# Both feed-forward products of a transformer step as seven block products with the middle layer in DRAM

## The chip, the cores and the metric

The kernel runs on one core of one Trainium2 chip. A core has five engines that each work through a queue of their own in order: TensorE (PE, matrix products), VectorE (DVE), ScalarE (ACT), GpSimd (POOL) and SyncE (SP), which issues the transfers between DRAM and the on-chip memory. The matrix products write to PSUM, eight banks of 512 float32 columns on each of 128 partitions. The metric is the time on the device of one run, in microseconds, median of three runs; lower is better.

## The reference

One layer of a hybrid network over 1152 tokens (128 sample tokens, then 1024 prompt tokens) of width 1024: recurrent mixers, cross attention over a memory, a feed-forward of width 4096, and a final norm. The part that matters here:

```python
def rms_norm(x, w):
    xf = x.astype(jnp.float32)
    y = xf * lax.rsqrt(jnp.mean(xf * xf, axis=-1, keepdims=True) + EPS)
    return (y * w.astype(jnp.float32)).astype(x.dtype)
```

and, in each layer, `x + squared_relu_mlp(rms_norm(x, norm_ffn_w), w_ff1, w_ff2)`, where the feed-forward multiplies by `w_ff1` (1024 x 4096), takes max(0, .) squared, and multiplies by `w_ff2` (4096 x 1024). At the end comes `rms_norm(x, norm_final_w)`.

## The kernel before

The features lie on the 128 partitions and the tokens along the free axis, in three blocks of 384 (`BW`). Every large product is made in three matmuls: each operand is split into a high part and the rest, and `mm3` adds high x high (L206), high x rest of the tokens (L207) and rest of the weights x high (L208) in PSUM. The split of a weight chunk of 128 x 1024 is a cast on ScalarE (L187) and a subtraction on VectorE (L188); `load_w` does both, and the chunk itself comes by one transfer of 512 KB (L177).

A `Driver` writes the program: it runs one stream of dense products and, between its steps, pieces of other tasks that are due. That, with the priority of some instructions, settles the order of each engine's queue before the run. Most large tiles live in 34 equal slots (`NSLOT`); a tile can only be written when its slot's last use is over.

The stages: the mixers until about 690 us, then the output projection, the attention and its projection `wo`, until about 1063 us, then the feed-forward until 1872 us, then the end of the final norm. While `wo` runs, `ffn_pre` makes the normalised input of the feed-forward block by block: `norm_split` (L1196 to L1200) multiplies by the norm's weight, splits, squares, and adds the squares on GpSimd; the factor 1/rms of each token is applied later, to the products. `ff1` multiplies one of 32 chunks of 128 features by the three blocks, and `relu2` applies the factor and max(0, .) on VectorE (L1447), squares on ScalarE (L1448) and splits the result into two slots. After every four chunks, `ff2` adds that group's part of the second product, through `ff2_unit` (L1475), to the residual in the slots `x1`. There are eight groups; the last is done by `ff2_last`, in blocks of 384, 512 and 256 tokens, with the final norm's sums (L1490, L1493) and `final` (L1507, L1512, L1514, output at L1517) behind each block. The middle layer never leaves the chip.

## Time and profile before

| | |
|---|---|
| median of three runs | 1884.41 us (1883.89 to 1886.3) |
| profiled execution, span | 1885.5 us |
| mean granted TensorE clock | 0.993 |
| TensorE busy | 1847.3 us, 98% |
| VectorE busy | 1011.8 us, 54% |
| ScalarE busy | 660.8 us, 35% |
| GpSimd busy | 224.8 us, 12% |
| moved by DMA | 167.61 MB, mean 89 GB/s |

The profile is one execution. An engine's busy time is what its instructions took; a wait is idle time before an instruction, with the instruction that released it. Matmuls overlap: one is listed with its whole length, 0.34 us at 384 columns, while the next starts sooner, so the rate is read from the starts. The granted clock is the share of TensorE's full 2.4 GHz.

### The profile page before, as it was taken

Reading aid. Unit: us, or ns where it says so; the run is one execution under the profiler, and the core shown is the slowest. Engines: PE = TensorE matmul, PEld = TensorE weight load, DVE = VectorE, ACT = ScalarE, POOL = GpSimd, SP = SyncE. Lnnn points to the kernel's source line nnn. Section 1 sums busy time; section 2 is a strip of 40 time slices with the busy share of each in tenths; the row PEclk is TensorE's granted clock in tenths of the full one; section 3 lists DMA queues with packets and bytes.
Section 4 is the critical chain, followed back from the end, with each engine's and each line's share of the span. In section 5 each row is a group of like instructions: output and inputs, shape, how many; then the busy total and the mean of one; then the engine's idle time right before and its main releaser. Section 6 shows DMA issues by size and latency. Waiting matters only on the chain.

```text
span 1885.5 us, 29978 instructions
## 1 busy us (share of the span) xinstructions
PE 1847.3 (98%) x12182; PEld 1796.4 (95%) x12182; DVE 1011.8 (54%) x2008; ACT 660.8 (35%) x1476; POOL 224.8 (12%) x262
## 2 busy tenths in 40 slices
...
DVE  6867756756756676436677533333333333333346
...
POOL 3123223123113012010012100000000000000003
...
DMA packets 73825, 167.61 MB, mean 89 GB/s; under 512 B 21680, under 2 KB 39760, under 8 KB 73688
## 3 DMA queue, kind: packets, MB, share of 16 engines
...
q14 instruction: 41, 0.34, 0.1%
q10 hardware_dynamic: 296, 0.19, 0.0%
...
## 4 chain that ended last, share of the span: by engine, by line
PE 86%; DVE 6%; ACT 3%; DMA 2%; issue 1%; POOL 1%; SPq 0%; DVEq 0%; ACTq 0%; POOLq 0%
PE d L206 25%; PE d L208 24%; PE d L207 24%; DVE y L583 1%; DVE wl L188 1%; DVE B L730 1%; DMA wr<-wout 1%; ACT xh L327 1%; DVE B L731 1%; ACT wh L187 1%; DMA R<-rowD 1%; DVE up L596 1%; PE st L960 1%; DMA xf<-xT 0%; ACT junk L672 0%
## 5 line engine op out<-in xcount | busy, mean ns | idle before, releaser
L187 ACT CAST wh<-wr 128x1024 fp32r<-128x1024 f32 x184 | 193.2, 1050 | 628.8 <-PE d L207 574.0
L206 PE MATMUL d<-xh,wh 128*128 128x384 f32 x944 | 342.3, 363 | 1.3 <-DVE k L428 0.6
L208 PE MATMUL d<-xh,wl 128*128 128x384 f32 x944 | 321.1, 340 | 0.3 <-DVE wl L188 0.3
L207 PE MATMUL d<-xl,wh 128*128 128x384 f32 x944 | 318.3, 337 | 0.0
L188 DVE TENSOR_TENSOR wl<-wr,wh 128x1024 fp32r<-128x1024 f32 x183 | 225.7, 1234 | 97.6 <-ACT wh L187 97.3
L206 PE MATMUL d<-hh,wh 128*128 128x384 f32 (+2 forms) x768 | 259.9, 338 | 0.0
L206 PE MATMUL d<-fh,wh 128*128 128x384 f32 x768 | 259.5, 338 | 0.0
L208 PE MATMUL d<-fh,wl 128*128 128x384 f32 x768 | 258.4, 336 | 0.0
L207 PE MATMUL d<-fl,wh 128*128 128x384 f32 x768 | 258.2, 336 | 0.0
L207 PE MATMUL d<-hl,wh 128*128 128x384 f32 (+2 forms) x768 | 257.9, 336 | 0.0
L208 PE MATMUL d<-hh,wl 128*128 128x384 f32 (+2 forms) x768 | 257.7, 336 | 0.0
L1475 DVE TENSOR_TENSOR x<-d,x 128x384 f32<-128x384 f32 (+1 forms) x200 | 107.5, 541 | 220.3 <-PE d L208 220.3
L206 PEld LDWEIGHTS d<-xh,wh 128*128 128x128 f32 x944 | 179.1, 190 | 7.4 <-issue 5.3
L207 PEld LDWEIGHTS d<-xl,wh 128*128 128x128 f32 x944 | 179.4, 190 | 1.6 <-issue 1.4
L208 PEld LDWEIGHTS d<-xh,wl 128*128 128x128 f32 x944 | 178.3, 189 | 0.8 <-DVE wl L188 0.6
L1447 DVE SCALAR_TENSOR_TENSOR sq<-d,rf 128x384 f32<-128x384 f32 x96 | 53.5, 558 | 174.3 <-PE d L208 171.0
L207 PEld LDWEIGHTS d<-hl,wh 128*128 128x128 f32 x768 | 144.3, 188 | 1.3
L208 PEld LDWEIGHTS d<-hh,wl 128*128 128x128 f32 x768 | 144.2, 188 | 1.4
L206 PEld LDWEIGHTS d<-hh,wh 128*128 128x128 f32 x768 | 144.2, 188 | 1.3
L207 PEld LDWEIGHTS d<-fl,wh 128*128 128x128 f32 x768 | 144.2, 188 | 0.0
L206 PEld LDWEIGHTS d<-fh,wh 128*128 128x128 f32 x768 | 144.1, 188 | 0.0
L208 PEld LDWEIGHTS d<-fh,wl 128*128 128x128 f32 x768 | 144.1, 188 | 0.0
...
## 6 DMA issues: line engine op xcount, KB each, us to landing
...
```

Source lines behind the costliest of these rows:

```text
L187: nc.scalar.copy(wh, raw)
L188: (nc.gpsimd if pool else nc.vector).tensor_tensor(wl, raw, wh, ALU.subtract)
L206: mm(ps, lhsT=lh, rhs=rh, start=start, stop=False)
L207: mm(ps, lhsT=lh, rhs=rl, start=False, stop=False)
L208: mm(ps, lhsT=ll, rhs=rh, start=False, stop=stop)
L327: nc.scalar.activation(xh, x(k), AF.Copy, scale=wc)
L583: v.scalar_tensor_tensor(y[:, :n], up[:, j:j + n], self.convw[:, c, j:j + 1], y[:, :n], ALU.mult, ALU.add)
L596: v.scalar_tensor_tensor(up[:, P:T], up[:, P:T], 1.0, y[:, 152:1176], ALU.add, ALU.mult)
L730: v.tensor_tensor(tmp[:, :, :i + 1], X[:, :, :i + 1], bc(NP[:, 0:i + 1, i], [72, 16, i + 1], 1), ALU.mult)
L731: v.tensor_reduce(X[:, :, i], tmp[:, :, :i + 1], AX.X, ALU.add)
L1447: v.scalar_tensor_tensor(r, ps[:, :BW], 0.0, self.rf[:, s], ALU.max, ALU.mult)
L1475: self.nc.vector.tensor_tensor(x, ps[:, o:o + hi - lo], x, ALU.add)
```

## The change

Both feed-forward products are cut into 2 x 2 blocks of features, of summed index and of tokens, and each set of eight block products is replaced by seven (Strassen's scheme in Winograd's form). Tokens are taken in two halves of 576, each of two quarters of 288 (`Q`). Per unit, four sums of weight blocks are made on GpSimd (`wf_sums`), and each of the seven left factors is split anew on ScalarE and VectorE (`wf_split`), three products ahead.

First layer: a unit is a pair of feature tiles. Pairs 0 to 2 are done for the first half of the tokens alone, pairs 3 to 15 for both halves, then pairs 0 to 2 for the second half: 19 units. `ff_in` makes the weighted input on ScalarE and the squares' sum on GpSimd, writes the residual to DRAM (`x2D`), and `ff_split` makes four sums of input blocks on GpSimd and seven splits for each half. A unit's seven products go to three double banks X, Y, Z of PSUM and are taken out by `evac`; `up_out` makes the four sums that the second layer wants of the hidden blocks and writes them to DRAM (`hD`), four transfers for a unit.

Second layer: a unit is a pair of output tiles, four for each of five groups of pairs (`GROUPS`). `hid_in` reads a group's hidden blocks back and splits them (L1690, L1691), as the last unit of the group before frees its slots. The residual comes back from DRAM into `E`, and every product is added to it (L1738). Pairs 14 and 15 (`PLAIN`) are kept as they are and go through `ff2_last`, whose 288 matmuls are the old ones. The final norm writes each feature tile by a transfer of its own, 32 in place of 12. `ffn_pre`, `ff1`, `relu2` and `ff2` are gone. Some constants move to a pool that ends with the mixers; before the feed-forward nothing else is changed.

The core of the diff:

```diff
+Q = 288
+HALVES = 2
+GROUPS = ((3, 4, 5), (6, 7, 8), (9, 10, 11), (0, 1, 2), (12, 13))
+PLAIN = (14, 15)
+FIRST = 3
+UP = (("P6", "s2", "T2", "Y"), ("P1", "A11", "B11", "X"), ("P5", "s1", "T1", "Z"), ("P7", "s3", "T3", "Y"),
+      ("P2", "A12", "B21", "X"), ("P4", "A22", "T4", "Y"), ("P3", "s4", "B22", "Z"))
+DOWN = (("P6", "s2", "T2", "Y"), ("P5", "s1", "T1", "Z"), ("P1", "A11", "B11", "X"), ("P3", "s4", "B22", "Z"),
+        ("P7", "s3", "T3", "Y"), ("P2", "A12", "B21", "X"), ("P4", "A22", "T4", "Y"))
...
+    def ff_in(self, b):
...
+        for k in range(KT):
+            yield from self.until(f"wo{b}{k}")
+            x = self.x1[b](k)
+            wc = self.prm[:, P_WFFN + k:P_WFFN + k + 1]
+            sq = acc if k == 0 else self.t(self.m4, [P, BW], "sq", bufs=2)
+            nc.scalar.activation(sq, x, AF.Square)
+            for q, lo, hi, to in self.pieces(b):
+                t = self.xq[q // 2][f"B{1 + k // 4}{1 + q % 2}"]
+                nc.scalar.activation(t[:, k % 4, to:to + hi - lo], x[:, lo:hi], AF.Copy, scale=wc)
+            if k:
+                nc.gpsimd.tensor_tensor(acc, acc, sq, ALU.add)
+            yield 0.0, 0.3
+        for g in range(3):
+            nc.sync.dma_start(self.x2D[:, 3 * g:3 * g + (3 if g < 2 else 2), s], self.x1g[b][g])
...
+    def ff_split(self, a):
...
+        tt = nc.gpsimd.tensor_tensor
+        tt(x["T1"], x["B12"], x["B11"], ALU.subtract)
+        tt(x["T2"], x["B22"], x["T1"], ALU.subtract)
+        x["T3"] = x.pop("B12")
+        tt(x["T3"], x["B22"], x["T3"], ALU.subtract)
+        tt(x["T4"], x["B21"], x["T2"], ALU.subtract)
+        yield 0.0, 3.0
+        for _, _, n, _ in UP:
+            yield from self.room(2)
+            h, l = self.S([P, 4, Q], F32R, "xqh"), self.S([P, 4, Q], F32R, "xql")
+            self.split(x[n], h, l)
+            self.F()
+            self.xo[a][n] = (h, l)
+            yield 0.0, 1.0
+            self.done.add(f"xo{a}{n}")
...
+    def wf_raw(self, src, n):
+        r1 = self.t(self.wp, [P, 1024], "wr")
+        r2 = self.t(self.m3, [P, 1024], "wr2", bufs=2)
+        with self.hp():
+            for r, a in zip((r1, r2), src):
+                self.nc.sync.dma_start(r[:, :2 * n], a)
+        return {"A11": r1[:, :n], "A12": r1[:, n:2 * n], "A21": r2[:, :n], "A22": r2[:, n:2 * n]}
+    def wf_sums(self, q, n):
+        def tt(o, a, b, op):
+            q[o] = self.t(self.m3, [P, 512], "ws", bufs=4)[:, :n]
+            with self.hp():
+                self.nc.gpsimd.tensor_tensor(q[o], q[a], q[b], op)
+        tt("s1", "A21", "A22", ALU.add)
+        tt("s2", "s1", "A11", ALU.subtract)
+        yield
+        tt("s3", "A11", "A21", ALU.subtract)
+        tt("s4", "A12", "s2", ALU.subtract)
+        yield
+    def wf_split(self, t, n):
+        if self.wi % 2 == 0:
+            self.wfh = self.t(self.wp, [P, 1024], "wh", F32R)
+            self.wfl = self.t(self.wp, [P, 1024], "wl", F32R)
+        o = 512 * (self.wi % 2)
+        self.wi += 1
+        h, l = self.wfh[:, o:o + n], self.wfl[:, o:o + n]
+        with self.hp():
+            self.nc.scalar.copy(h, t)
+            self.nc.vector.tensor_tensor(l, t, h, ALU.subtract)
+        return h, l
+    def seven(self, units, tasks):
...
+        for u, (_, _, products, body) in enumerate(units):
+            start(u + 1)
+            for x in tasks.get(u, ()):
+                self.dr.spawn(x)
+            next(body)
+            for j, p in enumerate(products):
+                ahead(i + 3)
+                if j in (3, 5):
+                    add(u + 1)
+                yield from body.send((p, ready[i]))
+                ready[i] = None
+                i += 1
...
+    def products(self, ps, w, x, n, blocks, first):
+        (wh, wl) = w
+        for a in blocks:
+            for k in range(n):
+                h, l = x(a, k)
+                s = slice(k * P, k * P + P)
+                self.mm3(ps[:, a, :Q], wh[:, s], wl[:, s], h, l, first and k == 0, k == n - 1, not first)
+                yield 3 * Q / 2180.0
...
+        def relu2(t, ps, n):
+            v.scalar_tensor_tensor(t, ps, 0.0, rf[:, bs, n], ALU.max, ALU.mult)
+            nc.scalar.activation(t, t, AF.Square)
+        def evac(name, o):
+            if name == "P1":
+                D, C = slot("D"), slot("C")
+                nc.scalar.copy(D[:, 1, bs], o)
+                v.tensor_tensor(C[:, 1, bs], bank["Y"][:, bs, :Q], D[:, 1, bs], add)
+            elif name == "P7":
+                B = slot("B")
+                v.tensor_tensor(B[:, 1, bs], o, H["D"][:, 1, bs], add)
+                v.tensor_tensor(H["C"][:, 0, bs], bank["Z"][:, bs, :Q], B[:, 1, bs], add)
+                relu2(H["C"][:, 0, bs], H["C"][:, 0, bs], 1)
+            elif name == "P2":
+                relu2(slot("A")[:, 0, bs], o, 0)
+            elif name == "P4":
+                v.tensor_tensor(H["B"][:, 0, bs], o, H["D"][:, 1, bs], add)
+                relu2(H["B"][:, 0, bs], H["B"][:, 0, bs], 0)
+            elif name == "P3":
+                t = H["D"][:, 0, bs]
+                v.tensor_tensor(t, o, H["C"][:, 1, bs], add)
+                relu2(t, t, 1)
+                for a in blocks:
+                    self.left[a] -= 1
+                    if not self.left[a]:
+                        self.F(14)
+                if not any(self.left):
+                    self.F()
+                    self.keep = 0
+                self.dr.spawn(self.up_out(pair, H, blocks), 0.0)
...
+    def up_out(self, pair, H, blocks):
...
+            tt = lambda o, a, b: v.tensor_tensor(o, a, b, ALU.subtract)
+            tt(A[:, 1, bs], D[:, 0, bs], A[:, 0, bs])
+            yield 0.0, 0.5
+            tt(C[:, 1, bs], C[:, 0, bs], A[:, 1, bs])
+            yield 0.0, 0.5
+            tt(D[:, 0, bs], C[:, 0, bs], D[:, 0, bs])
+            yield 0.0, 0.5
+            tt(B[:, 1, bs], B[:, 0, bs], C[:, 1, bs])
+            yield 0.0, 1.5
+            d = self.hD[pair]
+            for i, t in enumerate((C, A, D, B)):
+                q = slice(0, 1) if i == 2 else slice(0, 2)
+                nc.sync.dma_start(d[i][:, q, bs], t[:, q, bs])
...
+    def hid_in(self, g):
...
+        for i, names in ((0, ("B22", "T2")), (1, ("B11", "T1")), (2, ("T3",)), (3, ("B21", "T4"))):
+            step = 2 if i == 2 else 1
+            for j in range(0, len(pairs), step):
+                yield from self.room(3 + self.keep)
+                t = self.S([P, 2, 2, Q], F32, "ht")
+                self.live += 2
+                some = pairs[j:j + step]
+                for o, p in enumerate(some):
+                    if i == 2:
+                        nc.sync.dma_start(t[:, o], self.hD[p][2][:, 0])
+                    else:
+                        nc.sync.dma_start(t, self.hD[p][i])
+                use = [((j + o, "T3"), o) for o in range(len(some))] if i == 2 else [((j, n), o) for o, n in enumerate(names)]
+                yield 0.0, 3.5
+                self.live -= 2
+                q = len(some) if i == 2 else 2
+                h = self.S([P, 2, 2, Q], F32R, "hh")
+                l = self.S([P, 2, 2, Q], F32R, "hl")
+                nc.scalar.copy(h[:, :q], t[:, :q])
+                v.tensor_tensor(l[:, :q], t[:, :q], h[:, :q], ALU.subtract)
+                self.F()
+                for key, o in use:
+                    hid[key] = (h[:, o], l[:, o])
+                    self.done.add(f"hid{g}{key[0]}{key[1]}")
+                yield 0.0, 0.5
...
+    def down(self, g, d):
...
+            with self.hp():
+                o = bank[b][:, :, :Q]
+                e1, e2 = self.E[2 * d], self.E[2 * d + 1]
+                f1 = self.fs[d // 2][:, d % 2]
+                add = lambda e, t: v.tensor_tensor(e, e if t is f1 else t, t if t is f1 else e, ALU.add)
+                if name == "P1":
+                    if g == 0:
+                        nc.scalar.copy(f1, o)
+                    else:
+                        add(f1, o)
+                for m, t in {"P6": ((e1, 1),), "P5": ((e2, 1),), "P3": ((e1, 1),), "P7": ((e2, 1),), "P2": ((e1, 0),),
+                             "P4": ((e2, 0),)}.get(name, ()):
+                    add(m[:, :, t], o)
+                if g == len(GROUPS) - 1 and name == "P4":
+                    for m, t in ((e1, 1), (e2, 0), (e2, 1)):
+                        add(m[:, :, t], f1)
+            if d == 3:
+                self.F({"P1": 2 * n, "P3": 2 * n, "P7": 2 * ((n + 1) // 2), "P4": 2 * n}.get(name, 0))
+        while got is not None:
+            got = yield step(*got)
...
+            units = [(p, (0,)) for p in range(FIRST)] + [(p, (0, 1)) for p in range(FIRST, 16)]
+            units += [(p, (1,)) for p in range(FIRST)]
...
+            for g in range(len(GROUPS)):
+                for d in range(4):
+                    if d == 3 and g + 1 < len(GROUPS):
+                        start[len(jobs)] = [self.hid_in(g + 1)]
+                    if d == 0 and g + 1 == len(GROUPS):
+                        start[len(jobs)] = [self.plain_in(hid), self.plain_w(ws)]
+                    src = A[f"wd{g}"][d].rearrange("p q n -> p (q n)")
+                    n = len(GROUPS[g]) * P
+                    jobs.append(((src[:, :2 * n], src[:, 2 * n:]), n, DOWN, self.down(g, d)))
+            ff = self.seven(jobs, start)
...
+            dense.close()
+            self.pf = ps.enter_context(tc.tile_pool(name="psf", bufs=4, space=PS))
+            dr.stream(ff)
```

What this makes of the queues, at three places. GpSimd first, as the feed-forward starts. Before, in the feed-forward it had nothing to do until the final norm's multiplications (`x` by `rp`):

```order
L1512 TENSOR_TENSOR x_1844_10370<-x_1844_10370,rp_17792 128x384 [waits DMAHW5_49]
L1512 TENSOR_TENSOR x_1844_10370<-x_1844_10370,rp_17792 128x384
L1512 TENSOR_TENSOR x_1984_11080<-x_1984_11080,rp_17797 128x128 [waits DMAHW1_49]
L1512 TENSOR_TENSOR x_1984_11080<-x_1984_11080,rp_17797 128x128
L1512 TENSOR_TENSOR x_1845_10372<-x_1845_10372,rp_17792 128x384 [waits DMAHW6_49]
```

After, around the first unit: `acc` is the squares' sum of the last block, `ws` a sum of weight blocks, `xq` a sum of input blocks, `csy` the power that gives 1/rms.

```order
L1452 TENSOR_TENSOR acc_11270<-acc_11270,sq_11591 128x384 [waits Activation_49,Pool_49]
L1501 TENSOR_TENSOR ws_11714<-wr_2076_11624 128x512 [waits DMAHW1_49,DVE_49]
L1501 TENSOR_TENSOR ws_11716<-ws_11714,wr_11623 128x512 [waits DMAHW7_49,DVE_49,Pool_49]
L1452 TENSOR_TENSOR acc_11270<-acc_11270,sq_11638 128x384 [waits Activation_49]
L1501 TENSOR_TENSOR ws_11768<-wr_11623,wr_2076_11624 128x512 [waits DVE_49]
L1473 TENSOR_TENSOR xq_11651<-xq_10791,xq_11650 128x1152 [waits Activation_49]
L1475 TENSOR_TENSOR xq_10789<-xq_10791,xq_10789 128x1152
L1476 TENSOR_TENSOR xq_11652<-xq_10790,xq_11651 128x1152 [waits Pool_49]
L175 TENSOR_TENSOR csy_11703<-cst_11701,nhalf 128x3 [waits DVE_49]
```

The power now stands behind the last addition, a weight sum and three sums of 1152 columns.

VectorE in the middle of the old first layer: `sq` is a product taken out, `hl` the rest of a hidden tile, `wl` the rest of a weight chunk.

```order
L165 TENSOR_TENSOR hl_14735<-sq_14762,hh_14734 128x384 [waits Activation_49]
L1447 SCALAR_TENSOR_TENSOR sq_14792<-d_14767,rf_10762 128x384 [waits DVE_49,PE_49]
L165 TENSOR_TENSOR hl_14735<-sq_14793,hh_14734 128x384 [waits Activation_49]
L1447 SCALAR_TENSOR_TENSOR sq_14823<-d_14798,rf_10762 128x384 [waits DVE_49,PE_49]
L188 TENSOR_TENSOR wl_14832<-wr_14829,wh_14831 128x1024 [waits DMAHW7_49,Activation_49]
L165 TENSOR_TENSOR hl_14735<-sq_14824,hh_14734 128x384 [waits Activation_49]
```

After, where the third group of pairs follows the second, from the evacuation of the new group's first product, P6, on: `E` and `fs` take products, `hl` is the rest of a hidden tile that was read back (1152 columns, three for B11 and T1, then two for T3).

```order
L1738 TENSOR_TENSOR E_15112<-Y_17071,E_15112 128x2x288 [waits PE_49]
L1520 TENSOR_TENSOR wl_17094<-ws_17011,wh_17093 128x384 [waits Activation_49]
L1520 TENSOR_TENSOR wl_17094<-ws_17009,wh_17093 128x384 [waits Activation_49]
L1691 TENSOR_TENSOR hl_17098<-ht_17078,hh_17097 128x1152 [waits DMAHW6_49,Activation_49]
L1691 TENSOR_TENSOR hl_17104<-ht_17101,hh_17103 128x1152 [waits DMAHW7_49,Activation_49]
L1691 TENSOR_TENSOR hl_17110<-ht_17107,hh_17109 128x1152 [waits DMAHW0_49,Activation_49]
L1738 TENSOR_TENSOR E_15122<-Z_17113,E_15122 128x2x288 [waits PE_49]
L1738 TENSOR_TENSOR fs_15303<-X_17138,fs_15303 128x576 [waits PE_49]
L1520 TENSOR_TENSOR wl_17163<-wr_16877,wh_17162 128x384 [waits Activation_49]
L1520 TENSOR_TENSOR wl_17163<-wr_2670_16878,wh_17162 128x384 [waits DMAHW1_49,Activation_49]
L1691 TENSOR_TENSOR hl_17155<-ht_17120,hh_17154 128x1152 [waits DMAHW2_49,DMAHW1_49]
```

The three splits of B11 and T1 stand between the evacuations of P6 and P5, and the split of T3 behind that of P1 and two weight splits.

SyncE in the old feed-forward issues one weight chunk after another:

```order
L177 DMA wr_16458<-wff 128x1024 [waits DMAHW6_49,DVE_49]
L177 DMA wr_16559<-wff 128x1024 [waits DMAHW7_49,DVE_49]
L177 DMA wr_16649<-wff 128x1024 [waits DMAHW0_49,DVE_49]
L177 DMA wr_16739<-wff 128x1024 [waits DMAHW1_49,DVE_49]
L177 DMA wr_16829<-wff 128x1024 [waits DMAHW2_49,DVE_49]
```

After, at the same change of group, `ht` is a hidden tile read back and `wr` the weights of the next unit:

```order
L1683 DMA ht_17078<-hD_102 128x1152 [waits PE_49]
L1683 DMA ht_17101<-hD_103 128x1152 [waits PE_49]
L1683 DMA ht_17107<-hD_104 128x1152 [waits DMAHW0_49,PE_49]
L1681 DMA ht_17120<-hD_102 128x576 [waits DMAHW1_49,PE_49]
L1681 DMA ht_17120<-hD_103 128x576 [waits DMAHW2_49]
L1494 DMA wr_17282<-wd 128x768 [waits DMAHW3_49,DVE_49,Pool_49]
L1494 DMA wr_2735_17283<-wd 128x768 [waits DMAHW4_49,DVE_49]
L1681 DMA ht_17173<-hD_104 128x576 [waits DMAHW5_49,PE_49]
L1683 DMA ht_17203<-hD_102 128x1152 [waits DMAHW6_49,PE_49]
```

Two weight loads that wait for VectorE now stand between the second and the third part of T3.

## Rows read from the trace of the kernel before

**Rows 1.** Page, parts 1 and 2: busy shares, and tenths in 40 slices.
```profile
PE 1847.3 (98%) x12182; PEld 1796.4 (95%) x12182; DVE 1011.8 (54%) x2008; ACT 660.8 (35%) x1476; POOL 224.8 (12%) x262
...
DVE  6867756756756676436677533333333333333346
...
POOL 3123223123113012010012100000000000000003
```

**Rows 2.** Windows: stretch, length, busy us (count) per engine, clock, DMA share, GB/s.
```profile
1100.00:1200.00 100.00, 100.00 (x573) 100.00 (x572) 36.06 (x56) 20.49 (x32) 0.00 (x0) 1.00 0.13 43
...
1700.00:1800.00 100.00, 100.00 (x573) 100.00 (x573) 35.72 (x56) 20.48 (x32) 0.00 (x0) 1.00 0.13 43
```

**Rows 3.** Timeline, TensorE (start, us): 18 matmuls of 256 columns, then a weight load.
```profile
1859.32 0.28 PE L206 MATMUL d<-hh,wh 128*128 128x256 f32 x1
1859.43 0.28 PE L207 MATMUL d<-hl,wh 128*128 128x256 f32 x1
...
1861.34 0.28 PE L208 MATMUL d<-hh,wl 128*128 128x256 f32 x1
...
1872.16 0.19 PEld L207 LDWEIGHTS d<-hl,wh 128*128 128x128 f32 x1
```

**Rows 4.** Groups by form: line, operation, shapes, count, busy us, mean ns, idle before.
```profile
L188 DVE TENSOR_TENSOR wl<-wr,wh 128x1024 fp32r<-128x1024 f32 x132 | 161.6, 1225 | 66.5 <-ACT wh L187 66.4
L1475 DVE TENSOR_TENSOR x<-d,x 128x384 f32<-128x384 f32 x184 | 102.6, 558 | 220.3 <-PE d L208 220.3
...
L187 ACT CAST wh<-wr 128x1024 fp32r<-128x1024 f32 x132 | 138.6, 1051 | 471.1 <-PE d L207 438.3 <-issue 20.8 <-DMA wr<-wout 6.3
L164 ACT CAST hh<-sq 128x384 fp32r<-128x384 f32 x96 | 49.4, 515 | 3.0
...
L157 POOL TENSOR_TENSOR csy<-cst,nhalf 128x3 f32<-128x3 f32 x10 | 9.2, 920 | 873.0 <-DVE cst L249 873.0
L911 POOL TENSOR_TENSOR v<-v,soy 128x1152 f32<-128x1152 f32 x4 | 8.5, 2115 | 3.6 <-DVE soy L160 3.6
```

**Rows 5.** Timeline, VectorE and GpSimd: an addition beside VectorE's splits; one split before it.
```profile
1046.00 0.61 DVE L1197 SCALAR_TENSOR_TENSOR fl<-x,prm,fh 128x384 fp32r<-128x384 f32 x1
...
1062.29 1.23 DVE L188 TENSOR_TENSOR wl<-wr,wh 128x1024 fp32r<-128x1024 f32 x1 [0.40 <-ACT wh L187]
1063.43 1.38 DVE L1197 SCALAR_TENSOR_TENSOR fl<-x,prm,fh 128x384 fp32r<-128x384 f32 x1
...
1063.33 1.06 POOL L1200 TENSOR_TENSOR acc<-acc,sq 128x384 f32<-128x384 f32 x1 [3.14 <-ACT sq L1198]
```

**Rows 6.** Timeline, TensorE around a wait of 3.03 us, and windows behind it.
```profile
38.16 0.34 PE L226 MATMUL d<-xl,wh 128*128 128x384 f32 x1
41.52 1.62 PE L257 MATMUL bc<-cst,rsc 128*128 128x128 f32 x6 [3.03 <-DVE rsc L160]
...
43.58 0.52 PE L225 MATMUL d<-xh,wh 128*128 128x384 f32 x1
43.90 0.52 PE L226 MATMUL d<-xl,wh 128*128 128x384 f32 x1
...
43.00:44.00 1.00, 1.00 (x5) 1.00 (x5) 0.31 (x1) 0.82 (x3) 0.00 (x0) 0.50 0.00 0
```

**Rows 7.** A lone weight load: its issue, the windows of its bytes; a full window.
```profile
1392.62 0.33 SPq L177 DMA_DIRECT2D wr<-wff  x1
...
1395.00:1395.50 0.50, 0.50 (x4) 0.50 (x4) 0.23 (x1) 0.23 (x1) 0.00 (x0) 1.00 0.67 270
...
680.00:700.00 20.00, 20.00 (x116) 20.00 (x115) 12.45 (x18) 11.19 (x19) 3.48 (x3) 1.00 0.92 318
```

**Rows 8.** Waits of SyncE's queue: for what, us in total, times, longest.
```profile
SPq L177 <- DVE wl L188: 1108.2, 135, 18.2
```

**Rows 9.** Timeline of the end: last matmul, the norm's sum and its broadcast.
```profile
1872.40 0.28 PE L208 MATMUL d<-hh,wl 128*128 128x256 f32 x1
...
1875.43 0.60 PE L269 MATMUL st<-cst,acc 128*128 128x1 f32 x4 [2.75 <-DVE acc L1493]
...
1877.81 1.20 PE L257 MATMUL bc<-cst,rsf 128*128 128x128 f32 x4 [1.78 <-DVE rsf L160]
```

356 lines of the change are left out of this document (241 added, 115 removed).

## The prediction

> **What bounds the kernel now.** The page's busy shares come first [rows 1]: TensorE is busy 98% of the span, VectorE 54%, and in the right half of the forty slices, where the feed-forward runs, VectorE's digit is 3 and GpSimd's 0. The windows of that stage [rows 2] say it sharper: in 100 us TensorE issues 573 matmuls of 384 columns and never waits, VectorE works 36 us, ScalarE 20, GpSimd nothing, and the DMA engines move 43 GB/s. So this stage is bound by the number of matmuls times their spacing, 100 / 573 = 0.1745 us, and whatever removes columns there is worth its full time, as long as the other engines' new work fits beside it. That "as long as" is the whole question, since the change takes much of that room.
>
> **What is removed.** The old products that go are 32 chunks x 3 blocks x 8 x 3 = 2304 matmuls for the first layer and 7 groups x 8 x 3 x 4 x 3 = 2016 for the second: 4320 of 384 columns, 4320 x 0.1745 = 753.8 us. The last group (288 matmuls in blocks of 384, 512 and 256) stays. New are 16 pairs x 2 halves x 7 x 4 x 3 = 2688 and 14 pairs x 4 x 7 x 2 x 3 = 2352, together 5040 of 288 columns. No row has 288. The nearest are 256 columns, (1861.34 - 1859.32) / 17 = 0.1188 us from start to start [rows 3], and 384 at 0.1745; the line between them gives 0.1327. 5040 x 0.1327 = 668.8, so **85.0 us go**. The bounds are narrow: if 288 cost a proportional part of 384 (0.131) it would be 94, if it cost a proportional part of 256 (0.1337) it would be 80. Weight loads don't set this spacing: a 256-column matmul has its own load too [rows 3].
>
> **What the other engines get.** Durations by size come from pairs of rows [rows 4]: VectorE 0.558 us at 384 elements and 1.225 at 1024, so 0.46 at 288, 0.69 at 512, 0.76 at 576 and 1.36 at 1152; ScalarE 0.515 and 1.051, so 0.62 at 512 and 1.16 at 1152; GpSimd at best 1.06 at 384 [rows 5] and 2.12 at 1152, so about 1.25 at 512.
>
> - A unit with both halves: TensorE 168 x 0.1327 = 22.3 us. VectorE 7 weight splits x 0.69, 9 evacuations and 4 differences x 0.76 = 14.7. GpSimd 4 x 1.25 = 5.0. Transfers in and out about 3.1 MB, 139 GB/s, where a window at full load moved 318 [rows 7]. It fits, and I followed the waits of slots and weights through the order and found none that comes late: 13 such units at no cost.
> - A unit with one half (three at the start, three at the end of the first layer): TensorE 11.15, VectorE 7 x 0.69 + 13 x 0.46 = 10.8. That is full.
> - A unit of the second layer with three pairs: TensorE 16.7 (2.39 per product), VectorE 9.2; with two pairs 11.15 (1.59 per product) against about 10.5.
>
> Here a row decides something. A GpSimd addition began at 1063.33 while VectorE still ran a split; VectorE's next operation, recorded from 1063.43, ended at 1064.81, 0.42 us after the addition had ended at 1064.39, and is listed with 1.38 us where the one at 1046.00 took 0.61: the two did not run side by side [rows 5]. The Trainium skill ("SBUF — State Buffer", section "SBUF: two separate sides") says that VectorE operations with two SBUF inputs and GpSimd operations take one pair of ports in turn, each for its whole length; the trace agrees, by the 0.42 us just named. In a one-half unit 7 x 0.69 + 7 x 0.46 = 8.1 us of VectorE's work read two SBUF tiles; with GpSimd's 5.0 in turn that is 13.1 against 11.15 of TensorE, **2 us lost per unit**. If both ran side by side it would be nothing, and the sum below about 12 us less. In the units with both halves (10.1 + 5.0 against 22.3) it costs nothing either way.
>
> **Where TensorE will wait.** Old cover is gone at the places where a tile must be made before the next product, and the order shows what stands ahead of it in each queue.
>
> 1. Start. The first unit needs 1/rms of the tokens early, and TensorE's broadcast of it stands in its queue behind about 8.5 us of products. GpSimd reaches the power for it (0.92) only behind two weight sums, an addition and three sums of 1152: 2.5 + 1.06 + 6.4 + 0.9 = 11 [rows 4, 5], with the norm's small operations and the copy out of PSUM 13.5: a wait of 5. Behind it VectorE has 1.36 x 2 before the next weight split (a wait of 3.5), then five more splits of 1.36, six weight splits and the differences before the next unit's first copy (6.5). With 1 for the change of PSUM pools, 2 for the ports and 2 x 2 for the second and third unit: **22 (15 to 28)**.
> 2. Last three units of the first layer, which share VectorE with three splits of 1.36 for the second: 3 x 2 + 4.1, less some slack: **8 (3 to 12)**.
> 3. First to second layer. The third load for T1 stands on SyncE behind the last unit's outputs, which wait for VectorE's four differences. About 6 us to that issue; a lone 512 KB load was issued at 1392.62 and still moved bytes after 1395.0 [rows 7], so 3 to land; 2.5 to cast and split. It is wanted after 3: 8.5, and 2.5 more for the later loads: **11 (7 to 14)**.
> 4. Three changes of group. The 34 slots are full, so the next group's loads wait until the last unit's products free slots, and their casts and splits fall into the first products. At P5, three casts stand behind two weight casts that wait for P6; cast, then split, three times, ends some 6 us after P6's end where 2.4 are there: a wait of 4 to 5. At P3, VectorE does P1's evacuation and two weight splits before T3's split, and the third part of T3 is loaded only behind two weight loads that wait for these very splits: 5 to 7. SyncE waits for VectorE's splits already [rows 8], but there only weights stand behind. Then 2 to 4 where B21 and the next unit's weights meet. That adds up to 11 to 16; since TensorE's order pulls products of the next unit ahead, I take 12 each, **36 (18 to 48)**.
> 5. The group of two pairs (VectorE full, GpSimd in turn with it) and the step into the last group: **8 (4 to 12)**.
> 6. Tail: the same chain from the last matmul to the end [rows 9], with 32 output transfers for 12: **1 (0 to 2)**.
> 7. Clock. After a wait of 3.03 us (38.16 to 41.52) the granted clock stood at 0.50, which is 1.2 GHz, through 44, and matmuls of 384 columns came 0.32 us apart instead of 0.1745 [rows 6]: about 1.4 us lost. Some 15 to 20 waits above are as long. Most of them end on VectorE's or a DMA's work, which runs on meanwhile and shortens the next wait: **5 (0 to 25)**.
>
> Sum of the waits 22 + 8 + 11 + 36 + 8 + 1 + 5 = 91 (47 to 141). 1885.5 - 85.0 + 91 = 1891.5 on the profiled execution's time. The median of the runs is 1.1 below it (1884.41 against 1885.5), so **1890 us**: the gain is paid back in waits.
>
> **Rivals.**
> - *The changes stay hidden (faster).* Place: items 1, 3 and 4. If slots come free a product earlier than I read and the T1 and T3 tiles are split before TensorE arrives, only the low ends remain, 47: 1885.5 - 85 + 47 - 1.1 = 1846. For it: VectorE has 45% of the second layer free, so no throughput is missing, only order. Against it: the loads behind the weights in SyncE's queue. It decides at 85 us of waits.
> - *The clock doesn't recover (slower).* Every wait of 3 us is followed by a stretch at 1.2 GHz [rows 6], and nothing absorbs it: 20 x 1.4 = 28 instead of 5, 1913. The Trainium skill ("TensorE: Matmul & The Clock Gate", section "HAM oscillation — how this bites in real kernels") tells of a kernel whose products wait for a transfer each time and start throttled each time. By that rule this one is the case; the trace of before agrees for single waits, and shows none in close succession.
> - *Nothing is saved.* If 288 columns were spaced like 384, 5040 x 0.1745 = 879.5 and the time near 2100. The 256-column rows speak against it.
>
> **How the numbers follow.** Forecast 0.53 (1868 to 1908), hidden 0.25, clock 0.20, nothing saved 0.02. The measurement tells 0.2% from no change, so same is 1880.6 to 1888.2. Faster: 0.25 and a fifth of the forecast's case, 0.36. Same 0.12. Slower 0.52. The range runs from the hidden case to somewhat above the clock's, 1845 to 1920.
>
> **What would show it.** Matmuls of 288 columns 0.133 us apart in the middle of the first layer, with TensorE never idle there: the 85. Idle before `bc` and before the second unit: item 1. Idle at the second and fourth product after each change of group, ended by splits at L1691: item 4. A granted clock below 1 there: item 7. I am wrong if the second layer has few waits over 2 us, or if the 13 full units wait.

## The result, and the profile after

The changed kernel takes **1933.23 us** (median of four runs, 1931.49 to 1936.79) where the kernel before took 1884.96 in four runs beside it: a ratio of 1.026 (95% interval 1.0245 to 1.0274), 48 us slower. The forecast was 1890, 6 us above the kernel before, with a range of 1845 to 1920 and a chance of 0.52 for slower: the direction was little better than an even bet, and the size lies outside the range. The profiled execution took 1931.49, its span is 1929.7 us against 1885.5 before, so 44.2 us of span have to be placed.

First the page, busy shares and tenths in 40 slices, as [rows 1] shows them for before:

```profile
PE 1805.9 (94%) x12902; PEld 1734.8 (90%) x12902; DVE 1268.3 (66%) x2293; ACT 771.0 (40%) x1689; POOL 462.8 (24%) x426
...
PE   7999999999999999999999699999987979898897
...
PEclk9999999999999999999999799999998989899999
```

VectorE's share rose from 54% to 66% and GpSimd's busy time doubled. TensorE's row tells where to look: it is at 9 through the first layer except for one 6 at its start, and from about 1400 us on, at that layer's end and in all of the second, 8 and 7 come again and again, with the clock's digit at 8 in three of these slices. Windows of both layers, columns as in [rows 2]:

```profile
1140.00:1240.00 100.00, 100.00 (x756) 100.00 (x756) 69.20 (x90) 34.03 (x56) 27.89 (x18) 1.00 0.35 126
...
1640.00:1660.00 20.00, 13.19 (x67) 11.83 (x68) 10.50 (x11) 5.12 (x7) 3.10 (x2) 0.78 0.38 137
```

In the middle of the first layer TensorE never waits. Around one change of group, 1640 to 1660, it issues 67 matmuls in 20 us where the spacing of the first window allows 151. That spacing is read from the timeline, from the first matmul of a full unit (168 matmuls) to the first of the next:

```profile
1147.40 0.29 PE L225 MATMUL Y<-xqh,wh 128*128 128x288 f32 x1
...
1169.67 0.29 PE L225 MATMUL Y<-xqh,wh 128*128 128x288 f32 x1
```

(1169.67 - 1147.40) / 168 = 0.1326 us, where 0.1327 had been read off the line between the two sizes of [rows 2, 3]. The stretch that the products took before runs from the first product of the old first layer to the first of the old last stage:

```profile
1061.13 0.33 PE L206 MATMUL d<-fh,wh 128*128 128x384 f32 x1
...
1818.90 0.34 PE L206 MATMUL d<-hh,wh 128*128 128x384 f32 x1
```

With these the whole difference can be laid out. I call **loss** of a unit the time from its first matmul of 288 columns to the first of the next unit, less 0.1326 us for each matmul. A **slowed** matmul is one whose next starts 0.2 to 0.3 us behind it; the last column has what the slowed ones of a place took above 0.1326, which is part of the loss.

| place | predicted | measured | of it in slowed matmuls |
|---|---|---|---|
| products of the two layers | -85.0 | 5040 x 0.1326 = 668.3 for a stretch that held 757.8 before (1061.13 to 1818.90): -89.5 | |
| start (first three units, and the first product, 3.5 later than before) | 22 | 27.1 + 3.5 = 30.6 | 4.2 |
| 13 units with both halves | 0 | 0.0 | 0.0 |
| last three one-half units | 8 | 11.4 | 2.4 |
| first to second layer (first group) | 11 | 22.3 | 3.5 |
| three changes of group | 36 | 19.5 + 20.3 + 18.7 = 58.5 | 14.9 |
| last group of two pairs, and the step out of it | 8 | 10.3 | 1.3 |
| end, from the first matmul of the last stage | 1 | 66.6 as before: 0 | |
| clock | 5 | in the rows above | 26.3 |

The losses sum to 133.1, and 133.1 - 89.5 = 43.6; the other 0.5 are three matmuls of the last stage that come before the last of the second layer. (4320 x 0.1745 is 753.8, 3.9 less than the stretch before held. Some 1.2 of this are the norm's twelve small matmuls, which the changed kernel has in its 27.1. The rest is spacing: (757.8 - 1.2) / 4320 = 0.1751, while the 573 matmuls of a window in [rows 2] include those that had begun before it.) The end is unchanged: behind the last matmul the same chain as in [rows 9], 13.1 us to the end of the span.

```profile
1916.61 0.28 PE L227 MATMUL f<-hh,wl 128*128 128x256 f32 x1
1919.21 0.58 PE L288 MATMUL st<-cst,acc 128*128 128x1 f32 x4 [2.32 <-DVE acc L1825]
1921.47 1.22 PE L276 MATMUL bc<-cst,rsf 128*128 128x128 f32 x4 [1.69 <-DVE rsf L178]
```

What TensorE waits for in the second layer, from 1460 to 1860 us (line, releaser, us in total, times, longest):

```profile
PE Z L225 <- ACT hh L1690: 11.5, 6, 2.7
PE Z L226 <- DVE hl L1691: 11.1, 10, 3.8
PE Y L225 <- ACT hh L1690: 11.1, 3, 4.0
PE Y L226 <- DVE hl L1691: 6.3, 11, 1.6
```

All four are the cast and the split of hidden tiles that have been read back. For one change the chain of work that ended last (from 1634 to 1660) says what stands behind the cast:

```profile
1651.42 0.14 PE Z L225
1652.05 4.96 DMA ht<-hD
1657.04 0.68 ACT hh L1690
1657.74 0.77 DVE hl L1691
1658.55 0.61 PE Y L226
```

This group's first product began at 1634.95. 17 us later, at 1652.05, SyncE issues the load of the third pair's part of T3, which the fifth product, P7, multiplies; it is used 4.96 us after its issue. SyncE's queue at the same place (start, length of the issue, line) shows why it is so late:

```profile
1624.79 0.33 SPq L1683 DMA_DIRECT2D ht<-hD  x1
1625.22 4.34 SPq L1494 DMA_DIRECT2D wr<-wd  x2
1629.65 1.87 SPq L1683 DMA_DIRECT2D ht<-hD  x4
1631.62 0.95 SPq L1681 DMA_DIRECT2D ht<-hD  x2
1651.15 0.81 SPq L1494 DMA_DIRECT2D wr<-wd  x2
1652.05 0.38 SPq L1681 DMA_DIRECT2D ht<-hD  x1
1652.53 1.34 SPq L1683 DMA_DIRECT2D ht<-hD  x3
```

Seven hidden loads go out in the last ten microseconds of the old group, as its slots come free; the last four stand behind two weight loads (`wr`), which wait until 1651.15 for a weight split, and that stands on VectorE behind hidden splits of this very group and behind the evacuations of P5 and P1, which came late because of those splits.

### The profile page after: what moved, and what is told of

It is laid out like the page before. It is cut to its first block, busy times and chain, and to the rows that moved or that the text cites. A ratio compares the mean times of both kernels' runs of the same rounds, so it can differ in the third digit from the quotient of the medians.

```text
span 1929.7 us, 32888 instructions
## 1 busy us (share of the span) xinstructions
PE 1805.9 (94%) x12902; PEld 1734.8 (90%) x12902; DVE 1268.3 (66%) x2293; ACT 771.0 (40%) x1689; POOL 462.8 (24%) x426
## 3 DMA queue, kind: packets, MB, share of 16 engines
q8 instruction: 102, 1.67, 0.4%
## 4 chain that ended last, share of the span: by engine, by line
PE 76%; DVE 9%; ACT 4%; DMA 4%; issue 3%; POOL 2%; SPq 1%; DVEq 0%; ACTq 0%; POOLq 0%
PE d L225 10%; PE d L227 10%; PE d L226 10%; PE Y L226 4%; PE Y L225 4%; PE Y L227 4%; PE Z L226 3%; PE Z L227 3%; PE Z L225 3%; PE X L225 3%; PE X L226 3%; PE X L227 3%; DMA ht<-hD 2%; DVE wl L1520 1%; DVE hl L1691 1%
## 5 line engine op out<-in xcount | busy, mean ns | idle before, releaser
L1519 ACT CAST wh<-ws 128x512 fp32r<-128x512 f32 (+2 forms) x156 | 82.5, 552 | 199.7 <-issue 79.6
L225 PE MATMUL Y<-xqh,wh 128*128 128x288 f32 x384 | 116.5, 303 | 6.7 <-DVE h L1596 5.3
L227 PE MATMUL Y<-xqh,wl 128*128 128x288 f32 x384 | 115.1, 300 | 0.6 <-DVE wl L1520 0.6
L226 PE MATMUL Y<-xql,wh 128*128 128x288 f32 x384 | 115.1, 300 | 0.0
L225 PE MATMUL Y<-hh,wh 128*128 128x288 f32 x336 | 101.7, 303 | 13.6 <-ACT hh L1690 11.1
L1520 DVE TENSOR_TENSOR wl<-ws,wh 128x512 fp32r<-128x512 f32 (+2 forms) x156 | 110.3, 718 | 2.6 <-ACT wh L1519 2.2
L226 PE MATMUL Y<-hl,wh 128*128 128x288 f32 x336 | 102.1, 304 | 6.3 <-DVE hl L1691 6.3
L227 PE MATMUL Y<-hh,wl 128*128 128x288 f32 x336 | 101.4, 302 | 0.3 <-DVE wl L1520 0.3
L1691 DVE TENSOR_TENSOR hl<-ht,hh 128x1152 fp32r<-128x1152 f32 (+1 forms) x51 | 78.6, 1551 | 25.4 <-ACT hh L1690 25.2
L1520 DVE TENSOR_TENSOR wl<-wr,wh 128x512 fp32r<-128x512 f32 (+2 forms) x117 | 79.1, 685 | 19.3 <-ACT wh L1519 19.1
```

The costliest lines, as they stand in the source:

```text
L225: mm(ps, lhsT=lh, rhs=rh, start=start, stop=False, skip_group_check=more)
L226: mm(ps, lhsT=lh, rhs=rl, start=False, stop=False, skip_group_check=more)
L227: mm(ps, lhsT=ll, rhs=rh, start=False, stop=stop, skip_group_check=more)
L1519: self.nc.scalar.copy(h, t)
L1520: self.nc.vector.tensor_tensor(l, t, h, ALU.subtract)
L1691: v.tensor_tensor(l[:, :q], t[:, :q], h[:, :q], ALU.subtract)
```

## The experiments

Each kernel is the changed one with the edit shown; a few build on an earlier experiment and say so. The table has the time, the time of the first product of 288 columns, and the losses as defined above ("changes" are the groups between the first and the last, three or, with groups of two pairs, five; the last column ends at the first matmul of the next stage). A single run can differ by 5 us from another of the same kernel, and even the first product, before which most edits change nothing, came at 1064.6 to 1068.1. So small differences are read from the losses.

| kernel | us | first product | first layer | first group | changes | last group |
|---|---|---|---|---|---|---|
| changed kernel | 1933.2 | 1064.6 | 38.5 | 22.3 | 58.5 | 8.8 |
| e1_warm | 1932.3 | 1066.9 | 38.3 | 21.9 | 49.8 | 17.5 |
| e2_wq | 1917.4 | 1066.1 | 37.8 | 21.1 | 45.6 | 8.0 |
| e3_nosum | 1917.3 | 1068.1 | 29.6 | 22.6 | 51.4 | 6.7 |
| e4_reuse | 1863.7 | 1065.2 | 38.8 | 21.9 | -0.6 | 0.4 |
| e5_nosplit | 1925.4 | 1067.3 | 30.1 | 22.3 | 57.8 | 9.0 |
| e6_first0 | 1896.8 | 1072.7 | 13.0 | 28.4 | 32.8 | 12.6 |
| f_outq | 1905.6 | 1065.3 | 35.6 | 14.9 | 42.8 | 7.9 |
| f_two | 1858.4 | 1065.1 | 37.1 | 12.2 | 3.8 | 2.2 |
| g_two_first0 | 1846.1 | 1072.3 | 13.2 | 16.6 | 3.6 | 2.8 |
| g_two_tail1 | 1846.8 | 1071.5 | 12.5 | 19.0 | 4.1 | 2.2 |
| h_two_late | 1864.3 | 1065.6 | 37.0 | 11.7 | 10.6 | 1.7 |
| h_norm_late | 1931.0 | 1065.5 | 38.2 | 21.4 | 58.2 | 8.9 |
| i_nodma | 1866.2 | 1066.5 | 37.6 | 21.3 | 1.4 | 1.4 |
| best_first0 | 1846.0 | 1071.4 | 12.6 | 17.6 | 3.5 | 2.2 |
| best_norm | 1844.8 | 1067.2 | 18.7 | 16.9 | 4.1 | 2.1 |

### Is it the read-back, the clock, the order of loads or GpSimd?

My theory was the forecast's: tiles read back come late, and the order in SyncE's queue makes them later. The rivals were the clock, and GpSimd's sums taking VectorE's time. Four kernels, one for each. **e4_reuse** leaves the read-back out: all groups multiply the first group's tiles.

```diff
+        if g:
+            self.hid[g] = self.hid[0]
...
+            return
```

> Groups 1 to 4 use the first group's hidden tiles again, nothing is read back for them (part of the computation is left out). It prices the changes of group as a whole: if they are nothing but the read-back, its splits and what the clock makes of it, 59 us of the three changes and 8 of the step into the last group go, to about 1865. If something else stalls the second layer (evacuations, weights), 30 us or less go.

Measured: 1863.72, 69.5 us less. The three changes lose nothing, the last group 0.4; the first layer and the first group are as before. So the price of the changes hangs on the read-back with its loads, casts and splits, and not on the order of products, evacuations or weights.

**e1_warm** keeps TensorE busy with matmuls into unused PSUM columns, 36 ahead of P5 and 55 ahead of P3. The first stand where TensorE waited; the others stand one product ahead of the second wait, which is before P7.

```diff
+            if d == 0 and g and name in ("P5", "P3"):
+                for i in range(36 if name == "P5" else 55):
+                    nc.tensor.matmul(bank["Z"][:, 0, Q:512], lhsT=w[0][:, :P], rhs=hid[0, "T2"][0][:, 0, :512 - Q],
+                                     start=name == "P5", stop=name == "P5", skip_group_check=True)
             yield from self.products(bank[b], w, x, n, both, first)
```

> At each change of group, 36 extra matmuls of 224 columns (about 3.8 us) are put ahead of the second product P5 and 55 (about 5.8 us) ahead of P3, into columns that nobody reads, so that TensorE stays busy where it waited. In the changed kernel 260 of the 288-column matmuls came about 0.24 us apart instead of 0.1326, 27 us together, 17 of them in the four changes of group. If the clock is a price of its own there, the granted clock stays at 1.00 and the time falls by 8 to 15 us. If the waits are set by splits and transfers alone, the slow stretches only took the place of waiting: no more than 3 us either way.

Measured: 1932.31, the same time. Windows from 1540 to 1660 us of the changed kernel, then of this one:

```profile
1540.00:1660.00 120.00, 99.58 (x656) 94.11 (x655) 72.25 (x91) 35.23 (x54) 25.46 (x20) 0.91 0.38 137
```

```profile
1540.00:1660.00 120.00, 113.66 (x845) 111.32 (x844) 71.98 (x91) 36.75 (x56) 25.75 (x21) 0.97 0.39 137
```

The granted clock rose from 0.91 to 0.97, and each change lost 2.1 to 3.3 us less (58.5 to 49.8 together); in the last group the added matmuls were longer than the waits and cost as much again (8.8 to 17.5), so that the total didn't move. Slowed matmuls were not all prevented: at the three changes they fell from 14.9 us to 5.1. Of these 9.8 us 8.7 came back, so as far as this one run shows, what a slowed stretch costs there is nearly all lost time. Of some 19.5 us of a change about 3 went with the slowed matmuls that were prevented, and the 5.1 that were left are part of what remains.

**e2_wq** has GpSimd issue the second layer's weight loads, so that they no longer stand ahead of hidden loads on SyncE.

```diff
-                self.nc.sync.dma_start(r[:, :2 * n], a)
+                (self.nc.sync if n == 512 else self.nc.gpsimd).dma_start(r[:, :2 * n], a)
```

> The second layer's weight loads are issued by GpSimd instead of SyncE, so that the third part of T3 no longer stands behind them. If that order is the cause of the wait at P3 (about 9 us over its matmuls at each of three changes), 4 to 6 us go at each, 12 to 18 in all. If it is the landing of the loads under load or the splits on VectorE, the time stays within 4 us.

Measured: 1917.43. The three changes lose 45.6 instead of 58.5, 4.3 less each. The order on SyncE is worth that much and not the whole.

**e3_nosum** leaves out GpSimd's sums of weights (the products take an unsummed quarter).

```diff
-            q[o] = self.t(self.m3, [P, 512], "ws", bufs=4)[:, :n]
-            with self.hp():
-                self.nc.gpsimd.tensor_tensor(q[o], q[a], q[b], op)
+            q[o] = q[a]
```

> GpSimd makes no sums of weight blocks (the products use the plain blocks instead, so part of the computation is left out). If GpSimd's additions hold up VectorE in the units with one half, units 0 to 2 (27 us over their matmuls) and 16 to 18 (11 us) lose 10 to 20 us together; the changes of group lose little. If only the splits of the second half's input fill VectorE there, under 5 us go.

Measured: 1917.26. The first layer loses 8.9 less, 3.7 of it in the first three units and 5.2 in the last three, a little under the 10 to 20 expected; the changes, where little was expected, lose 7.1 less. What those sums last in the changed kernel, by groups of one form from 1060 to 1470 us (count, then busy us and mean ns):

```profile
L1501 POOL TENSOR_TENSOR ws<-wr,wr 128x512 f32<-128x512 f32 x19 | 31.7, 1671 | 32.2 <-DVE wl L1520 32.2
...
L1501 POOL TENSOR_TENSOR ws<-wr,ws 128x512 f32<-128x512 f32 x19 | 27.3, 1438 | 104.9 <-DVE wl L1520 104.9
```

I had taken 1.25 us from durations at 384 and 1152 columns [rows 4, 5]; they last 1.44 to 1.67. VectorE pays as well. Differences of hidden tiles from 1150 to 1400 us and hidden splits from 1545 to 1740 us, in the changed kernel and then in this one:

```profile
L1648 DVE TENSOR_TENSOR h<-h,h 128x576 f32<-128x576 f32 x44 | 43.1, 1009 | 4.1 <-ACT h L1590 3.8
L1691 DVE TENSOR_TENSOR hl<-ht,hh 128x1152 fp32r<-128x1152 f32 x25 | 40.7, 1645 | 3.0 <-ACT hh L1690 2.9
```

```profile
L1646 DVE TENSOR_TENSOR h<-h,h 128x576 f32<-128x576 f32 x44 | 31.8, 755 | 5.1 <-ACT h L1588 4.4
L1689 DVE TENSOR_TENSOR hl<-ht,hh 128x1152 fp32r<-128x1152 f32 x26 | 34.7, 1354 | 3.2 <-ACT hh L1688 2.9
```

Without the sums they last what the prediction had interpolated (0.76 and 1.36 us); with them 0.25 and 0.29 us more on average. Additions of a product from PSUM (`E<-Y,E`) last 0.755 and 0.756. That bears out the prediction's term for VectorE and GpSimd taking turns: it had priced it at some 12 us in the one-half units, and 8.9 went, whatever part of them is the sums' own lateness.

### Transfers or splits?

e4_reuse takes away the loads, the casts and the splits together. **i_nodma** takes away the loads alone, for all groups but the first: casts and splits stay and read a constant column; the slots of the tiles that are not loaded stay reserved, but nothing is written to them.

```diff
+                    if g:
+                        pass
-                    if i == 2:
+                    elif i == 2:
...
+                if g:
+                    t = bc(bc(self.prm[:, 0:1], [P, 2, 1], 2), [P, 2, 2, Q], 2)
                 nc.scalar.copy(h[:, :q], t[:, :q])
```

> The changed kernel, but groups 1 to 4 transfer no hidden tiles: their casts and splits read a constant column instead, in the same number and size, and still take their slots (part of the computation is left out). It parts transfers from splits in the 18 to 20 us that each change of group costs. e2_wq gave back 5 of them by the order on SyncE alone, e1_warm about 3 by the clock. If transfers and their landing are most of the rest, 10 to 14 us go at each of three changes, to about 1890. If casts and splits, queued behind slots and evacuations, are the rest, no more than e2_wq's 5 to 7 go, about 1910.

Measured: 1866.24. The changes lose 0.4 to 0.5 us each, as without any read-back. Window 1540 to 1660 of this kernel:

```profile
1540.00:1660.00 120.00, 119.86 (x901) 119.04 (x899) 88.13 (x122) 44.34 (x72) 35.80 (x28) 1.00 0.15 48
```

VectorE and ScalarE do their casts and splits (88 us of 120 for VectorE) and TensorE doesn't wait. So the 19.5 us of a change hang on the transfers: that they are issued late and take some 5 us, and that casts and splits queue up behind them in that order. Landing and order were not separated here, since without a transfer the casts also stand further ahead in their queues: at the change to the third group six of them run before its first product, and two in the changed kernel.

### What makes the loads late: the size of a group

A group of three pairs keeps 22 of the 34 slots for its hidden tiles, one of two pairs 14. **f_two**, built on e2_wq, has seven groups of two pairs and starts to read the next group back at the group's second unit instead of its last.

```diff
-GROUPS = ((3, 4, 5), (6, 7, 8), (9, 10, 11), (0, 1, 2), (12, 13))
+GROUPS = ((3, 4), (5, 6), (7, 8), (9, 10), (11, 12), (0, 13), (1, 2))
...
-                if d == 3 and g + 1 < len(GROUPS):
+                if d == 1 and g + 1 < len(GROUPS):
```

> As e2_wq, with seven groups of two pairs instead of five of three and two, and each group's read-back started two units earlier, since two groups' tiles then nearly fit the 34 slots. If late read-back is the cause of the waits at the changes, they fall from about 15 us to under 3 each (45 in all). But a unit of two pairs has 11.15 us of matmuls and some 10.5 us of VectorE, with the read-back's splits some 12.9, so that VectorE sets the pace: 1.7 us lost in each of 28 units, 48 in all. Sum about 1910 to 1925, lost in many small waits instead of few long ones.

Measured: 1858.43, 59 us less than e2_wq and less than the kernel before. The expectation fell: I had held VectorE too full for units of two pairs. By the prediction's own figures the 10.5 us that it took for such a unit are 8.3 and three additions that only the last group has; without these, and with the read-back's splits, it is 10.7, under TensorE's 11.15. One stretch, and SyncE's hidden loads from 1550 to 1612:

```profile
1560.00:1660.00 100.00, 99.35 (x749) 99.10 (x748) 91.33 (x142) 40.09 (x81) 41.06 (x53) 1.00 0.44 154
```

```profile
1554.30 12.74 SPq L1683 DMA_DIRECT2D ht<-hD  x6
1580.62 0.97 SPq L1681 DMA_DIRECT2D ht<-hD  x2
1598.90 12.32 SPq L1683 DMA_DIRECT2D ht<-hD  x6
```

VectorE is busy 91 us of 100 and TensorE 99. Each group has eight loads, in the program's order: four for B22 and B11, two for T3 (L1681), two for B21. So a row of six holds the last two of one group and the first four of the next. The group that begins at 1605.48 has its first four at 1556.18 to 1566.72, T3's two from 1580.62 on, and the last two at 1598.90 and 1600.36: all are issued 5 to 49 us ahead of it. In the changed kernel the last four of a group of three pairs went out 17 to 19 us into it.

Taking the weights off SyncE does not do this alone. In e2_wq, with groups of three pairs, the longest waits of SyncE's queue from 1470 to 1660 are for a slot's last product:

```profile
SPq L1683 <- PE X L227: 83.7, 4, 41.5
```

There only the first load goes out some 52 us ahead of its group; the second waits for a slot's last product until 10 us ahead, and the last leaves 18 us into the group.

**h_two_late** asks whether the early start or the small group did it: f_two with `d == 3` again.

> As f_two, but the read-back of the next group starts only with the last unit of a group, as in the changed kernel. It tells the two parts of f_two apart. If the early start is the cause of its gain (changes of group of about 1 us instead of 15), six changes of some 8 to 13 us come back, 1905 to 1935. If the smaller group alone does it, since its tiles leave room in the slots, it stays within 10 us of f_two's 1858.

Measured: 1864.28, only 5.8 more than f_two; its groups after the first lose 12.3 together, f_two's 6.0, and 6.8 of the 12.3 stand at the first change. The small group alone brings nearly all. Two rows of its loads, the last four of them before the group that begins at 1566.67 and the rest for the group after it:

```profile
1553.06 0.80 SPq L1681 DMA_DIRECT2D ht<-hD  x2
1560.13 12.74 SPq L1683 DMA_DIRECT2D ht<-hD  x6
```

Here too T3's loads leave 13 to 14 us ahead of the group and the last two, at 1560.13 and 1561.58, 5 us ahead. The place in the program matters little, since SyncE, with hidden loads alone in its queue, issues them as slots come free. With 14 slots for hidden tiles instead of 22 there is room for the next group while this one still runs. (More slots for groups of three pairs, which would test the room by itself, were not tried.)

### The step between the layers

**f_outq** is e2_wq with the hidden outputs of the one-half units issued by GpSimd, since SyncE's loads for the first group stand behind them.

```diff
-                nc.sync.dma_start(d[i][:, q, bs], t[:, q, bs])
+                (nc.gpsimd if blocks == (1,) else nc.sync).dma_start(d[i][:, q, bs], t[:, q, bs])
```

> As e2_wq (1917.4 us), and the hidden tiles of the last three units are written out from GpSimd's queue, so that the third load for T1 of group 0 doesn't stand behind them on SyncE. In e2_wq that load was issued at 1468.6, 8 us after the layer's last matmul, and the first unit of the second layer lost 16 us over its matmuls. If the place in the queue is the cause, 6 to 9 us of it go, to about 1910; if the loads wait for something else (slots, VectorE's differences), 2 or less.

Measured: 1905.56. SyncE's queue of e2_wq, then of this kernel:

```profile
1464.02 4.45 SPq L1660 DMA_DIRECT2D hD<-h  x4
1468.56 0.56 SPq L1683 DMA_DIRECT2D ht<-hD  x1
```

```profile
1456.84 0.84 SPq L1683 DMA_DIRECT2D ht<-hD  x2
```

A load for T1 that left at 1468.56 behind four outputs leaves by 1457.7. The first group loses 14.9 instead of 21.1: 6 of its 21 us were this order. The other 5 us of the gain are spread over the first layer (2.2) and the changes (2.8).

### The start of the first layer

The longest two waits there, from 1062 to 1112 us:

```profile
PE X L225 <- ACT h L1595: 8.6, 1, 8.6
PE bc L276 <- DVE rsf L178: 6.2, 1, 6.2
```

**h_norm_late** lets the broadcast of the third block's norm be asked for 22 us later, to see whether the 6.2 is a loss of its own.

```diff
-rf[:, s], f"rf{b}"), 3.0)
+rf[:, s], f"rf{b}"), 25.0 if b == 2 else 3.0)
```

> The changed kernel with one number changed: the norm's sum and broadcast for the third token block, which the first units with one half don't need, is written 22 us later into the program. TensorE waited 6.2 us for that broadcast in the first unit. If that wait is a cost of its own, 5 to 8 us go, to about 1925. If VectorE's backlog of splits sets the pace of units 0 to 2 anyway, the wait only moves to the next product and at most 2 us go.

Measured: 1931.01, the same. Its longest waits in the same stretch:

```profile
PE X L225 <- ACT h L1595: 9.5, 1, 9.5
PE Y L225 <- DVE h L1599: 4.1, 1, 4.1
PE Y L225 <- ACT wh L1519: 2.8, 1, 2.8
```

The wait before `bc` is gone and the loss is the same (38.2 for 38.5): the wait moved to the next tile that VectorE or ScalarE had not made. So the loss at the start is a backlog of work. In the chain to the norm GpSimd's sums of 1152 columns last more than the 2.12 I had taken:

```profile
1070.62 3.11 POOL L1473 TENSOR_TENSOR xq<-xq,xq 128x1152 f32<-128x1152 f32 x1
1073.69 2.63 POOL L1475 TENSOR_TENSOR xq<-xq,xq 128x1152 f32<-128x1152 f32 x1
```

**e5_nosplit** leaves out the second half's seven input splits (its products use the first half's).

```diff
+            if a == 1:
+                self.F()
+                self.xo[a][n] = self.xo[0][n]
+                self.done.add(f"xo{a}{n}")
+                continue
```

> The second half's seven input splits are left out, and the first half's tiles are used for both (part of the computation is left out); GpSimd's sums for it stay. The first two units lose 25 us over their matmuls in the changed kernel. If that is VectorE's backlog of seven splits of 1.36 us, 10 to 16 us go. If it is the chain of the norm through GpSimd, whose broadcast TensorE waits 6.2 us for, at most 4 us go.

Measured: 1925.39. The first layer loses 8.4 less, between the two cases of the expectation: the second unit 0.9 instead of 11.5, while the third rises from 2.4 to 6.0. The splits are most of the backlog, not all of it.

**e6_first0** does away with the one-half units: `FIRST = 0` makes 16 units with both halves.

> No units with one half: all sixteen pairs are done for both halves at once. The 27 us of units 0 to 2 and the 11 us of units 16 to 18 go, and the second half's sums and splits, some 13 us of work on GpSimd and VectorE, now stand ahead of the first unit's products. If one-half units are what fills VectorE, the time falls by 15 to 25 us, to about 1910. If the start costs the same wherever it stands, it stays within 6 us.

Measured: 1896.75, 36 us less. The first product comes 8 us later, since it now needs the second half's sums and splits too, and the first layer then loses 13.0 instead of 38.5: one-half units, which give the other engines half the time for the same weights, are the price. But the changes of group also lose 25.7 less, which nobody expected. In that kernel's order one weight load instead of two stands ahead of the third pair's part on SyncE, which goes out 12 us into a group instead of 17. And its hidden splits last 1.38 us instead of 1.65. Which of the two it is was not tested.

### A version that beats both

**g_two_first0** joins f_two and `FIRST = 0`, with groups (0,1), (2,3) and so on to (12,13). It has f_outq's queue too, which does nothing where no unit has one half, and its P6 is written to wait for one more residual tile. **g_two_tail1** takes the last pair's halves one after the other again, for more room at the step between the layers.

> What the last runs point to, put together: two pairs to a group with the read-back two units ahead (f_two, 1858.4 us), no units with one half (e6_first0, 36 us under the changed kernel), weights of the second layer and outputs of one-half units on GpSimd's queue. If the two gains lie in different places they add up, less what is lost where the first group's tiles can only be read back once the first layer's input tiles are free (27 us over the matmuls there in e6_first0, 10 in f_two): 1858 - 36 + 10, about 1832. If late read-back of the first group also delays the second, 1845 or more.

> As g_two_first0, but the last pair's halves come one after the other, so that half of the input's slots are free 11 us before the layer ends and the first group can be read back in them. If room is what holds the first group's read-back, the step between the layers shrinks by 8 to 15 us against g_two_first0, at a price of about 3 us for two one-half units. If the order of the transfers holds it, no gain.

Measured: 1846.05 and 1846.76. The one-half units at the end brought nothing (the first group lost 19.0 for 16.6). g_two_first0 was then timed again beside a version with the norm of the third block 9 us later:

```diff
-rf[:, s], f"rf{b}"), 3.0)
+rf[:, s], f"rf{b}"), 12.0 if b == 2 else 3.0)
```

> g_two_first0 again, timed against the kernel before on the same chip: 1846 us, a ratio of 0.979 to 0.981, faster than both kernels.

> g_two_first0 with the norm's sum and broadcast for the third token block written 9 us later. In g_two_first0 TensorE waits 5.3 us at the head of the first layer for GpSimd's sum of squares, which stands in its queue ahead of the products. If that is a cost of its own, 3 to 6 us go, to about 1842. If VectorE's splits of the input set the start, as h_norm_late showed for the one-half units, it stays within 2 us.

Measured: **best_first0 1846.0 (ratio to the kernel before 0.979, 0.978 to 0.981) and best_norm 1844.8 (0.978, 0.977 to 0.980)**: 39.5 and 41 us faster than before, 87 and 88 faster than the changed kernel, and no difference between the two that can be told: in best_norm the first product came 4.2 us earlier and the first layer lost 6.1 more, so the wait only moved again. Busy shares and slices of best_norm:

```profile
PE 1778.1 (96%) x12902; PEld 1720.0 (93%) x12902; DVE 1277.0 (69%) x2343; ACT 765.9 (42%) x1707; POOL 476.6 (26%) x502
...
PE   7999999999999999999999879999999799999997
```

Two dents are left: the first unit (16.8 in best_norm) and the first group (16.9).

## Why the prediction was wrong in size

- **The products: right.** 0.1327 was read off the line between 256 and 384 columns, 0.1326 measured. The old products were spaced 0.1751 instead of 0.1745, which makes the saving 2.8 us larger.
- **Thirteen full units at no cost: right**, 0.0 lost in each.
- **The steps that failed** are two of the sum, and each is some 21 us short. The **clock** was put at 5 (0 to 25) because a slowed stretch was held to shorten the next wait; slowed matmuls cost 26.3. And the **waits** of all places were put at 86; without the slowed matmuls they are 133.1 - 26.3 = 106.8, with most of the difference where tiles are read back: 11 + 36 forecast, 18.8 + 43.6 measured.
- **Clock: 5 forecast, 26.3 measured**, outside its bounds. 247 matmuls came about 0.24 us apart. Where e1_warm prevented 9.8 us of it, 8.7 came back, so the loss was not absorbed by the next wait, as I had assumed. This is the second rival's mechanism, and its 28 us come close. Its 1913 was still 20 short, since it added them to waits that were themselves too small.
- **Changes of group: 36 (18 to 48), measured 58.5.** I had put waits of 4 to 5 at P5, 5 to 7 at P3, 2 to 4 later, 11 to 16 each, and took 12 because products of the next unit could be pulled ahead. 14.9 of the 58.5 are slowed matmuls; the other 43.6 are 14.5 for each change, within the 11 to 16. So the sum of the waits held, and the deduction from it and the clock did not. The kind was right: the cover is gone, the loads stand behind weights in SyncE's queue (4.3 each by e2_wq), and without transfers nothing is left (i_nodma). The second wait stood at P7 and not at P3, since T3 is P7's tile and P3 uses B22. Two durations were short as well: I gave a load 3 us from its issue, from a lone one [rows 7], and this one took 4.96 to its use (1652.05 to 1657.04), with others in flight; and a hidden split lasted 1.65 for 1.36. Neither was tested by itself.
- **First to second layer: 11 (7 to 14), measured 22.3**, 3.5 of it in slowed matmuls. Outputs ahead of loads on SyncE was right and worth 6 (f_outq). The rest, some 15 us, I had as 5; 12 to 19 us stay in the versions with groups of two pairs, and were not taken apart.
- **Start: 22 (15 to 28) forecast, 30.6 measured**, 4.2 of it in slowed matmuls. The three waits came to 6.2 before `bc`, 0.6 before a weight split and 8.6 before the second unit, 15.4 together, for 5 + 3.5 + 6.5 = 15 forecast. h_norm_late shows why the sum held and the parts did not: they are one backlog, which comes out somewhere else if one of them is taken away. The durations on GpSimd were short: the sums lasted 2.6 to 3.1 for 2.12 and 1.44 to 1.67 for 1.25, and the first product is 3.5 later for a forecast of 1. The reading that VectorE and GpSimd "did not run side by side" [rows 5] was too strong for that row: the operation ended 0.42 us after the addition where it takes 0.61 alone, so part of it ran beside. That the two hold each other up is shown by e3_nosum.
- **Last one-half units: 8 (3 to 12), measured 11.4.** Within its bounds.
- **Last group of two pairs: 8, measured 10.3, for the wrong reason.** I had it lose because VectorE and GpSimd take turns in units of two pairs. f_two has seven such groups, and after the first group they lose 6.0 together. Most of the 10.3 stands in the group's first unit, at the change of group ahead of it.

The granted clock behind a wait, as in [rows 6] (columns as in [rows 2]; between them the wait before P7, from the timeline):

```profile
1645.00:1646.00 1.00, 1.00 (x6) 1.00 (x6) 0.58 (x1) 0.00 (x0) 0.00 (x0) 0.50 0.00 0
...
1657.76 0.50 PE L225 MATMUL Y<-hh,wh 128*128 128x288 f32 x1 [3.96 <-ACT hh L1690]
...
1660.00:1661.00 1.00, 1.00 (x6) 1.00 (x6) 0.00 (x0) 0.00 (x0) 0.00 (x0) 0.50 0.27 111
```

The Trainium skill ("TensorE: Matmul & The Clock Gate", section "HAM oscillation — how this bites in real kernels") tells of a kernel whose products wait for a transfer in every round and start each round throttled; the trace agrees in kind, with a granted clock of 0.50, 1.2 GHz, in these windows.

- **The first rival, that the changes stay hidden**, did not happen here, but its argument (VectorE has room, only order is missing) holds: with groups of two pairs the same work ran in 1858.4, and in 1844.8 without one-half units. That this is close to the 1846 it gave is luck: it had 18 us left at the changes and 7 at the first group, where best_norm loses 4.1 and 16.9.

Open: what in e6_first0's order takes 25.7 us off the changes; landing time against order of the casts in i_nodma; room in the slots tested by itself; and the 12 to 19 us that the first group still loses where groups have two pairs.
